# A hybrid encoder layer: two blocks at a time through the MLP, or one block with the next block's mixers between its steps

## The chip, the cores and the metric

The kernel runs on one core of a Trainium2 chip. The metric is the device time of one execution in microseconds (us). The engines are TensorE (PE, matmuls; PEld is its weight load), VectorE (DVE), ScalarE (ACT), GpSimd (POOL) and SyncE (SP), whose queue issues nearly all DMAs. SBUF is the memory on chip, PSUM the eight banks that matmuls write to.

## What is computed

One layer over 2,176 tokens of width 1024: a prompt of 2,048 and 8 running streams of 16 new frames. All data are fp32. The reference, cut down:

```python
h = rmsnorm(x, ln_mix)
q, k, v, u = split(h @ w_in)                  # 512, 128, 128, 512 columns
a = attention(q, k, v)                        # 8 heads, 2 kv heads; own 64-frame chunk + 128 frames before, sinks
b = multiscale_pool(u) * pool_scale           # trailing means over 2/4/8/16 frames minus u, 4 linear maps
x = x + concat(rmsnorm(a), rmsnorm(b)) @ w_out
x = x + square(relu(rmsnorm(x) @ w_up)) @ w_down          # 4096 hidden columns
x = x + sigmoid(rmsnorm(x) @ w_gate) * (p @ w_ple)
y = rmsnorm(x)                                # also returned: K, V and pooling rows
```

## The kernel before

Activations lie transposed, features on the 128 partitions and tokens along the row. The tokens are cut into six blocks (`BLOCKS`): block 0 has 256 (128 of the prompt and the 128 sample frames), the others 384. Blocks depend on each other only through the last 128 keys and values and the last 15 pooling rows of the block before.

Precision is kept by splitting each operand into a rounded part and the rest, hi and lo; each product is three matmuls (`mm3`, L113: hi x hi, lo x hi, hi x lo). `load_w` (L101) brings a 128 x 1024 weight tile of 512 KB by DMA into one of two raw buffers (`wraw`), ACT casts it to `whi` (L107), and DVE and POOL in turn subtract to give `wlo` (L110); there are three pairs of hi and lo. A tile feeds 24 matmuls for each block that uses it.

Phase A works off `SEQ_A`, an order written out by hand: for each block the norm and split of x (`P`), the input projection in 10 tiles (`I`), the attention in tiles of 128 queries (`A`; `S` for the sample streams of block 0), pooling (`K`), and the output projection (`O`), whose result x1 is written to HBM (`x1d`, L239). Blocks overlap in it. K and q have two buffers, the pooling input `ext` one.

Phase B takes the blocks in pairs, `SUPER = [(1, 2), (3, 4), (5, 0)]`. `mlp_start` reads x1 back, norms and splits it; `acc_load` reads it once more as the accumulator. `mlp` (L649) runs 16 chunks of two up-tiles and two down-tiles. Each weight tile is loaded and split once and used for both blocks. An up-tile ends in r = relu(ps) * rstd on DVE (L662), hi = square(r) on ACT (L666), r*r on DVE (L667) and lo = r*r - hi on DVE (L668). A down-tile's eight outputs are added to the accumulator in SBUF by DVE (L682), 128 adds a block. PSUM tiles of the MLP rotate through seven banks. Then come `gate` (L692) for each of the two, with the sigmoid and its multiplication, and `finish`, with the last norm and the output. All gate weights are split by POOL.

Instructions go out in an order that a planner in the compiler draws up from simulated times: an instruction later in the program can come ahead of one that is not ready. On the chip each engine then keeps its order.

Of the kernel before, what the change touches and what calls it, by code (L numbers as in the profile page):

```python
# [43 lines left out]
FCH = 2  # L44
# [8 lines left out]
C_W = 53  # L53


@with_exitstack
def hymba_step(ctx: ExitStack, tc: tile.TileContext, ins, outs):
# [34 lines left out]
    RING = ("mm", "sc", "tr", "mm", "sc", "tr", "pv")  # L92
    ring = [0]

    def ps_ring(nm):
        ring[0] += 1
        return ps_tile(RING[ring[0] % len(RING)], nm)

    cnt = [0]

    def load_w(src, ktiles, width=P, raw_bufs=2, hl_bufs=3, tag="w", pool=None, eng=None):  # L101
        pool = pool or wp
        raw = pool.tile([P, ktiles, width], F32, tag=tag + "r", name="wraw", bufs=raw_bufs)
        nc.sync.dma_start(out=raw, in_=src)
        hi = pool.tile([P, ktiles, width], F32R, tag=tag + "h", name="whi", bufs=hl_bufs)
        lo = pool.tile([P, ktiles, width], F32R, tag=tag + "l", name="wlo", bufs=hl_bufs)
        nc.scalar.copy(out=hi, in_=raw)  # L107
        cnt[0] += 1
        eng = eng or (nc.vector if cnt[0] % 2 else nc.gpsimd)
        eng.tensor_tensor(out=lo, in0=raw, in1=hi.bitcast(F32), op=ALU.subtract)  # L110
        return hi, lo

    def mm3(ps, whl, xs, first=True, last=True):  # L113
        n = len(xs)
        hi, lo = whl
        for i, (wsel, (xh, xl)) in enumerate(xs):
            nc.tensor.matmul(ps, lhsT=wsel(hi), rhs=xh, start=first and i == 0, stop=False)  # L117
            nc.tensor.matmul(ps, lhsT=wsel(lo), rhs=xh, start=False, stop=False)  # L118
            nc.tensor.matmul(ps, lhsT=wsel(hi), rhs=xl, start=False, stop=last and i == n - 1)  # L119

    def ks(xt, N, kk):
        return [((lambda t, k=k: t[:, k, :]), (xt[0][:, k, :N], xt[1][:, k, :N])) for k in kk]
# [5 lines left out]
    class SumSq:  # L128
        def __init__(self, n, acc=None):
            self.n = n  # L130
            self.acc = acc if acc is not None else tmp.tile([P, NMAX], F32, tag="sqa", name="sqa", bufs=5)
            self.first = True
            self.last_sig = None
# [31 lines left out]
        def rstd_load(self, dim, pstile):  # L165
# [27 lines left out]
    def row_tile(nm):  # L193
        return tmp.tile([P, NMAX], F32, tag="xr", name=nm, bufs=NXR)

    def load_norm(b, src, g, hl, rstd):
        N = BLOCKS[b]
        sq = SumSq(N)
        for k in range(KT):
            x = row_tile("x")[:, :N]  # L200
            nc.sync.dma_start(out=x, in_=src[:, k, :])
            gain_split(x, g + k, hl[0][:, k, :N], hl[1][:, k, :N], LOENG[k % len(LOENG)](nc))
            sq.add(x, eng=ADENG[k % len(ADENG)](nc))
        return rstd(sq)

    def hl_tile(nm, pool=xhl):
        h = pool.tile([P, KT, NMAX], F32R, tag="xh", name=nm + "h")
        l = pool.tile([P, KT, NMAX], F32R, tag="xl", name=nm + "l")
        return h, l
# [674 lines left out]
```

## Time and profile before

| | |
|---|---|
| median of 3 runs | 2560.95 us (2559.33 to 2562.33) |
| span of the profiled execution | 2563.4 us |
| busy: PE, DVE, ACT, POOL | 2438.7, 1814.0, 874.2, 827.8 us |
| DMA traffic | 249.17 MB, 97 GB/s on average |
| granted PE clock, mean | 0.977 |

A busy time is the union of an engine's instructions. Matmuls overlap in the record, so a busy PE is not yet a PE at its peak pace; the pace is seen by counting matmuls in a stretch. The idle time of an engine that is not the bound costs nothing.

### The profile page before, as it was taken

The page shows a single profiled execution, that of the slowest core. Times are in us where ns is not written, and L with a number is a line of the kernel's source. Part 1 is how long each engine was busy: PE and PEld are TensorE (multiplying, and loading weights), DVE is VectorE, ACT ScalarE, POOL GpSimd, SP SyncE. Part 2 cuts the span into 40 slices and gives each one's busy share as a digit, 9 for nine tenths or more (in the row PEclk, how much of TensorE's full clock was granted, in tenths as well). Part 3 has the DMA queues.
Part 4 walks back from the last instruction along what each step waited for, and adds up shares of the span by engine and source line. Part 5 has one row for each costly group of instructions (what it writes and reads, how often), then busy time and mean ns, then how long its engine had stood idle before and what let it go on. Part 6 is the DMA issues. An engine that isn't in the chain of part 4 may idle for free.

```text
span 2563.4 us, 36604 instructions
## 1 busy us (share of the span) xinstructions
PE 2438.7 (95%) x14324; PEld 2361.4 (92%) x14324; DVE 1814.0 (71%) x3113; ACT 874.2 (34%) x1601; POOL 827.8 (32%) x548
## 2 busy tenths in 40 slices
PE   7889998999899999999998999999999899999986
PEld 7888888998799999999888999999988899999986
DVE  6769888888765555555889555555587966666687
ACT  5446655445421111111652111111165212221254
POOL 4634557454631111111381111111138211111134
PEclk8989999999999999999999999999999999999998
DMA  5424335433732222222244222221234422222223
GB/s 157 129 87 137 95 120 165 138 106 97 249 102 65 59 66 66 63 62 66 91 151 158 66 66 59 66 63 59 61 102 135 136 75 75 83 74 67 83 76 113
DMA packets 104892, 249.17 MB, mean 97 GB/s; under 512 B 19600, under 2 KB 55440, under 8 KB 104720
## 3 DMA queue, kind: packets, MB, share of 16 engines
q1 hardware_dynamic: 104176, 246.32, 31.4%
q8 instruction: 112, 1.84, 0.3%
q10 hardware_dynamic: 544, 0.52, 0.1%
q14 instruction: 60, 0.49, 0.1%
HBM read 228.44 MB, written 18.36 MB: 96 GB/s over the span
## 4 chain that ended last, share of the span: by engine, by line
PE 59%; DVE 10%; ACT 2%; DMA 2%; issue 1%; POOL 0%; SPq 0%; DVEq 0%; ACTq 0%; POOLq 0%
PE ps_dn L117 10%; PE ps_dn L118 10%; PE ps_dn L119 10%; PE ps_up L119 9%; PE ps_up L118 9%; PE ps_up L117 9%; DVE sqa L144 2%; DVE acc L714 1%; DVE x1l L191 1%; DVE x2l L191 1%; DMA x<-x1d 1%; DVE rs_t L159 1%; DMA xr<-in_xT 1%; ACT whi L107 1%; DVE acc L737 1%
## 5 line engine op out<-in xcount | busy, mean ns | idle before, releaser
L110 POOL TENSOR_TENSOR wlo<-wraw,whi 128x1024 fp32r<-128x1024 f32 (+1 forms) x245 | 533.0, 2182 | 1466.9 <-ACT whi L107 1452.1
L107 ACT CAST whi<-wraw 128x1024 fp32r<-128x1024 f32 (+1 forms) x395 | 377.1, 968 | 999.8 <-issue 578.5
L682 DVE TENSOR_TENSOR acc<-ps_dn,acc 128x384 f32<-128x384 f32 (+1 forms) x768 | 389.6, 530 | 167.9 <-PE ps_dn L119 166.9
L117 PE MATMUL ps_dn<-hh,whi 128*128 128x384 f32 (+1 forms) x1536 | 500.0, 327 | 4.5 <-DVE r L662 4.5
L119 PE MATMUL ps_up<-x1l,whi 128*128 128x384 f32 (+1 forms) x1536 | 501.0, 326 | 1.2 <-DVE x1l L191 1.2
L117 PE MATMUL ps_up<-x1h,whi 128*128 128x384 f32 (+1 forms) x1536 | 501.4, 327 | 0.7 <-ACT x1h L190 0.7
L118 PE MATMUL ps_up<-x1h,wlo 128*128 128x384 f32 (+1 forms) x1536 | 501.9, 327 | 0.0
L118 PE MATMUL ps_dn<-hh,wlo 128*128 128x384 f32 (+1 forms) x1536 | 499.4, 327 | 0.0
L119 PE MATMUL ps_dn<-hl,whi 128*128 128x384 f32 (+1 forms) x1536 | 488.0, 326 | 0.0
L117 PEld LDWEIGHTS ps_dn<-hh,whi 128*128 128x128 f32 x1536 | 290.8, 189 | 5.1 <-DVE r L662 5.1
L119 PEld LDWEIGHTS ps_up<-x1l,whi 128*128 128x128 f32 x1536 | 290.2, 189 | 2.0 <-DVE x1l L191 1.5
L117 PEld LDWEIGHTS ps_up<-x1h,whi 128*128 128x128 f32 x1536 | 290.1, 189 | 1.3 <-ACT x1h L190 1.0
L118 PEld LDWEIGHTS ps_up<-x1h,wlo 128*128 128x128 f32 x1536 | 290.3, 189 | 0.7 <-issue 0.6
L118 PEld LDWEIGHTS ps_dn<-hh,wlo 128*128 128x128 f32 x1536 | 290.8, 189 | 0.0
L119 PEld LDWEIGHTS ps_dn<-hl,whi 128*128 128x128 f32 x1536 | 289.0, 189 | 0.2 <-DVE hl L668 0.2
L662 DVE SCALAR_TENSOR_TENSOR r<-ps_up,sqa 128x384 f32<-128x384 f32 x192 | 102.1, 535 | 254.2 <-PE ps_up L119 254.0
L667 DVE TENSOR_TENSOR r<-r 128x384 f32<-128x384 f32 x192 | 191.2, 998 | 97.4 <-ACT hh L666 97.4
L110 DVE TENSOR_TENSOR wlo<-wraw,whi 128x1024 fp32r<-128x1024 f32 x150 | 191.0, 1273 | 56.4 <-ACT whi L107 54.1
L666 ACT ACTIVATE hh<-r 128x384 fp32r<-128x384 f32 x192 | 96.3, 504 | 300.2 <-DVE r L662 300.0
L117 PE MATMUL ps_in<-xnh,whi 128*128 128x384 f32 (+1 forms) x472 | 162.9, 345 | 12.9 <-DVE z L561 5.5
L118 PE MATMUL ps_in<-xnh,wlo 128*128 128x384 f32 (+1 forms) x472 | 161.2, 342 | 2.7 <-POOL wlo L110 2.0
L119 PE MATMUL ps_in<-xnl,whi 128*128 128x384 f32 (+1 forms) x472 | 159.6, 339 | 0.0
(208 smaller groups left out, 3992.4 us busy)
## 6 DMA issues: line engine op xcount, KB each, us to landing
wraw<-in_w_up SPq DMA_DIRECT2D x96, 512.0 KB, 3.7
wraw<-in_w_down SPq DMA_DIRECT2D x96, 512.0 KB, 3.6
wraw<-in_w_in SPq DMA_DIRECT2D x59, 512.0 KB, 3.7
wraw<-in_w_out SPq DMA_DIRECT2D x48, 512.0 KB, 3.7
wraw<-in_w_gate SPq DMA_DIRECT2D x48, 512.0 KB, 3.6
x<-in_xT SPq DMA_DIRECT2D x40, 192.0 KB, 2.6
xr<-in_xT SPq DMA_DIRECT2D x40, 192.0 KB, 3.2
x1d<-xr SPq DMA_DIRECT2D x40, 192.0 KB, 2.1
```

The costliest lines, as they stand in the source:

```text
L107: nc.scalar.copy(out=hi, in_=raw)
L110: eng.tensor_tensor(out=lo, in0=raw, in1=hi.bitcast(F32), op=ALU.subtract)
L117: nc.tensor.matmul(ps, lhsT=wsel(hi), rhs=xh, start=first and i == 0, stop=False)
L118: nc.tensor.matmul(ps, lhsT=wsel(lo), rhs=xh, start=False, stop=False)
L119: nc.tensor.matmul(ps, lhsT=wsel(hi), rhs=xl, start=False, stop=last and i == n - 1)
L144: eng.tensor_tensor(out=o, in0=o, in1=t, op=ALU.add)
L159: V.tensor_tensor(out=u, in0=u, in1=y, op=ALU.mult)
L191: eng.scalar_tensor_tensor(out=lo, in0=src, scalar=c, in1=hi.bitcast(F32), op0=ALU.mult, op1=ALU.subtract)
L662: nc.vector.scalar_tensor_tensor(out=r, in0=ps, scalar=0.0, in1=rs1[b], op0=ALU.max, op1=ALU.mult)
L666: nc.scalar.activation(out=hh, in_=r, func=AF.Square)
L667: nc.vector.tensor_tensor(out=r, in0=r, in1=r, op=ALU.mult)
L682: nc.vector.tensor_tensor(out=acc[b][:, d, :N], in0=ps, in1=acc[b][:, d, :N], op=ALU.add)
```

## The change

Blocks now go through the MLP one at a time, 0 to 5. Block 0 first passes all its mixers and its output projection alone. Then, between the 64 steps (32 up-tiles, 32 pairs of down outputs) of block b's MLP, `run` places the steps of block b+1: reading and splitting x, 10 projection tiles, pooling groups, attention tiles in four steps each. In `gate` of block b the eight output tiles of block b+1 are placed; they start two tiles ahead of it. `out_proj` writes x1 into the accumulator and its split form on chip, so `x1d` and its transfers are gone.

The MLP has 8 chunks of four up-tiles; `w_down` is packed anew on the host so that a 512 KB tile holds two outputs for four hidden tiles. A block has 64 adds into the accumulator. r*r is on POOL.

Up and down weights are loaded and split for every block. The weights of input, output, gate and embedding projections are split at their first use, stored to HBM as hi and lo, and loaded as these from then on, two DMAs of 512 KB.

Large tiles of a block come from one pool of 16 buffers of 4 x 384 columns (`quad`). K and `ext` have one buffer. Of the PSUM banks four are for projections, MLP and gate, and one each for scores, transposes, values and sums. The adds of squares and the gate's add to the accumulator are on POOL; before, those of phase B were on DVE. The diff, cut to its core:

```diff
-SUPER = [(1, 2), (3, 4), (5, 0)]
-FCH = 2
+FCH = 4
+NCH = FT // FCH
+NQUAD = 16
+PS_BUFS = {"mm": 4, "sc": 1, "tr": 1, "pv": 1, "ms": 1}
...
-    def load_w(src, ktiles, width=P, raw_bufs=2, hl_bufs=3, tag="w", pool=None, eng=None):
+    def load_w(src, ktiles, key=None, raw_bufs=2, hl_bufs=3, tag="w", pool=None, eng=None):
...
+        if key in saved:
+            dh, dl = saved[key]
+            nc.sync.dma_start(out=hi.bitcast(F32), in_=dh)
+            nc.sync.dma_start(out=lo.bitcast(F32), in_=dl)
+            return hi, lo
...
+        if key is not None:
+            dh, dl = (dram.tile([P, ktiles, P], F32, name=f"ws{key}{c}") for c in "hl")
+            nc.sync.dma_start(out=dh, in_=hi.bitcast(F32))
+            nc.sync.dma_start(out=dl, in_=lo.bitcast(F32))
+            saved[key] = dh, dl
...
+    def out_proj(b, d):
...
+        a = acc_at(b, d)
+        nc.sync.dma_start(out=a, in_=xblk(xT, KT, b)[:, d, :])
+        whl = load_w(w_out[d], KT, f"out{d}")
...
+        gain_split(a, C_GFFN + d, at8(x1[b][0], d)[:, :N], at8(x1[b][1], d)[:, :N], nc.vector)
+        st_b["sq1"].add(a)
+        if d == KT - 1:
+            rs1[b] = st_b["sq1"].rstd_dve(D)
...
+        def up(c, j):
+            if j == 0:
+                hs[c] = quad("hh", F32R), quad("hl", F32R)
+            whl = load_w(w_up[c * FCH + j], KT)
+            ps = ps_tile("mm", "ps_up")[:, :N]
+            mm3(ps, whl, ks(x1[b], N, range(KT)))
+            r = row_tile("r")[:, :N]
+            nc.vector.scalar_tensor_tensor(out=r, in0=ps, scalar=0.0, in1=rs1[b], op0=ALU.max, op1=ALU.mult)
+            hh, hl = hs[c][0][:, j, :N], hs[c][1][:, j, :N]
+            nc.scalar.activation(out=hh, in_=r, func=AF.Square)
+            nc.gpsimd.tensor_tensor(out=r, in0=r, in1=r, op=ALU.mult)
+            nc.vector.tensor_tensor(out=hl, in0=r, in1=hh.bitcast(F32), op=ALU.subtract)
...
+            for i in range(2):
...
+                d = 2 * dp + i
+                ps = ps_tile("mm", "ps_dn")[:, :N]
+                mm3(ps, whl, [(i * FCH + j, (hh[:, j, :N], hl[:, j, :N])) for j in range(FCH)])
+                a = acc_at(b, d)
+                nc.vector.tensor_tensor(out=a, in0=ps, in1=a, op=ALU.add)
...
+    for b in range(nb):
+        nx = b + 1
+        side = []
+        if nx < nb:
+            side = prologue_steps(nx) + in_proj_steps(nx)
+            mix = [s for i in range(NPR[nx] // P) for s in attn_steps(nx, i)]
+            for i, s in enumerate(pool_steps(nx)):
+                mix.insert(3 * i, s)
+            side += [lambda: mixers(nx)] + mix + [lambda: out_rstd(nx)]
+        run(mlp_steps(b), side, 1, 62)
+        gate_rs(b)
+        G = [lambda d=d: gate(b, d) for d in range(KT)]
+        if nx < nb:
+            out_proj(nx, 0)
+            out_proj(nx, 1)
+            run(G, [lambda d=d: out_proj(nx, d) for d in range(2, KT)])
+        else:
+            run(G)
+        finish(b)
```

## Rows read from the trace of the kernel before

**Rows 1.** Busy time by stretch: us; busy us (count) per engine; clock, DMA share, GB/s.

```profile
0.00:200.00 200.00, 170.00 (x932) 156.74 (x933) 143.38 (x287) 94.24 (x203) 100.89 (x96) 0.89 0.45 125
200.00:640.00 440.00, 425.84 (x2427) 382.87 (x2427) 386.00 (x836) 242.59 (x561) 230.77 (x189) 0.99 0.40 123
640.00:724.00 84.00, 70.30 (x364) 64.98 (x362) 62.98 (x79) 37.16 (x63) 55.21 (x41) 0.94 0.67 231
724.00:1243.00 519.00, 519.00 (x2994) 518.70 (x2993) 310.32 (x489) 105.44 (x150) 77.75 (x32) 1.00 0.22 66
1243.00:1344.00 101.00, 89.26 (x493) 84.71 (x492) 87.48 (x104) 63.34 (x110) 73.99 (x46) 1.00 0.43 129
1344.00:1390.00 46.00, 37.05 (x191) 35.80 (x190) 44.82 (x84) 9.81 (x17) 8.29 (x3) 0.89 0.34 120
...
2025.00:2455.00 430.00, 430.00 (x2942) 430.00 (x2941) 281.22 (x484) 95.45 (x138) 74.71 (x31) 1.00 0.26 78
2455.00:2518.00 63.00, 54.81 (x312) 52.95 (x312) 49.39 (x67) 36.48 (x64) 35.49 (x21) 0.92 0.35 103
2518.00:2563.40 45.40, 25.50 (x178) 23.48 (x176) 33.55 (x56) 16.75 (x34) 16.55 (x11) 0.80 0.30 102
```

**Rows 2.** Score matmuls by tile, one of three such lines: ns, first and last.

```profile
L391 PE MATMUL ps_sc<-kh,qh x128: 271/280/579, 29.3 to 626.6; 64*128 64x256 f32 x120, 64*128 64x128 f32 x8
```

**Rows 3.** Weight splitting, groups by shape: count, busy us, mean ns, idle before.

```profile
L110 POOL TENSOR_TENSOR wlo<-wraw,whi 128x1024 fp32r<-128x1024 f32 x197 | 483.6, 2456 | 1440.6 <-ACT whi L107 1425.7 <-DVE sbuf L479 8.3 <-DMA wraw<-in_w_out 3.8
...
L107 ACT CAST whi<-wraw 128x1024 fp32r<-128x1024 f32 x347 | 359.1, 1048 | 999.8 <-issue 578.5 <-PE ps_up L119 245.8 <-PE ps_dn L119 55.1
...
L110 DVE TENSOR_TENSOR wlo<-wraw,whi 128x1024 fp32r<-128x1024 f32 x150 | 191.0, 1273 | 56.4 <-ACT whi L107 54.1 <-issue 0.6
```

**Rows 4.** Loads of up weights, from the page's DMA issues: KB, us to landing.

```profile
wraw<-in_w_up SPq DMA_DIRECT2D x96, 512.0 KB, 3.7
```

**Rows 5.** ACT in order of time, 20 to 46 us: first and last of six casts.

```profile
22.38 1.04 ACT L107 CAST whi<-wraw 128x1024 fp32r<-128x1024 f32 x1
...
43.41 1.04 ACT L107 CAST whi<-wraw 128x1024 fp32r<-128x1024 f32 x1 [1.10 <-DMA wraw<-in_w_in]
```

**Rows 6.** Busy time by stretch: the stretch with the densest DMA traffic.

```profile
684.00:688.00 4.00, 4.00 (x24) 3.84 (x23) 1.69 (x2) 1.33 (x2) 4.00 (x4) 1.00 1.02 421
```

**Rows 7.** Page's groups of the MLP steps, then two groups by shape.

```profile
L682 DVE TENSOR_TENSOR acc<-ps_dn,acc 128x384 f32<-128x384 f32 (+1 forms) x768 | 389.6, 530 | 167.9 <-PE ps_dn L119 166.9
...
L662 DVE SCALAR_TENSOR_TENSOR r<-ps_up,sqa 128x384 f32<-128x384 f32 x192 | 102.1, 535 | 254.2 <-PE ps_up L119 254.0
L667 DVE TENSOR_TENSOR r<-r 128x384 f32<-128x384 f32 x192 | 191.2, 998 | 97.4 <-ACT hh L666 97.4
...
L666 ACT ACTIVATE hh<-r 128x384 fp32r<-128x384 f32 x192 | 96.3, 504 | 300.2 <-DVE r L662 300.0
...
L668 DVE TENSOR_TENSOR hl<-r,hh 128x384 fp32r<-128x384 f32 x160 | 92.3, 578 | 4.1
...
L235 POOL TENSOR_TENSOR xr<-xr,ot 128x384 f32<-128x384 f32 x40 | 45.4, 1135 | 98.7 <-DVE ot L234 75.9 <-DMA xr<-in_xT 6.7 <-DVE st L415 6.3
```

**Rows 8.** In order of time around 729 us; then L667's min, median, max.

```profile
728.90 2.43 DVE L667 TENSOR_TENSOR r<-r 128x384 f32<-128x384 f32 x2
...
728.03 2.40 POOL L110 TENSOR_TENSOR wlo<-wraw,whi 128x1024 fp32r<-128x1024 f32 x1 [5.67 <-ACT whi L107]
...
L667 DVE TENSOR_TENSOR r<-r x192: 416/559/2440, 719.1 to 2442.4; 128x384 f32<-128x384 f32 x160, 128x256 f32<-128x256 f32 x32
```

**Rows 9.** Block 0's pooling and sample streams: count, ns, first and last start us.

```profile
L323 POOL TENSOR_TENSOR pw<-ext x2: 1177/2107/3037, 63.2 to 81.3; 128x960 f32<-128x960 f32 x1, 128x568 f32<-128x568 f32 x1
...
L468 PE MATMUL ps_ssc<-sbuf x16: 283/284/580, 115.3 to 170.1; 128*128 128x144 f32 x16
...
L491 ACT COPY asm<-ps_str x16: 201/207/209, 128.9 to 185.5; 64x64 f32<-64x64 f32 x16
```

**Rows 10.** PE in order of time near the end: the last gate matmul.

```profile
2549.37 0.28 PE L119 MATMUL ps_gt<-x2l,whi 128*128 128x256 f32 x1
```

More of the change, by code (lines that the diff above doesn't have):

```diff
@@ L115, in mm3, with ks @@
         hi, lo = whl
[L116 to L122, printed above, removed]
+        for i, (wi, (xh, xl)) in enumerate(xs):
+            nc.tensor.matmul(ps, lhsT=hi[:, wi, :], rhs=xh, start=first and i == 0, stop=False)
+            nc.tensor.matmul(ps, lhsT=lo[:, wi, :], rhs=xh, start=False, stop=False)
+            nc.tensor.matmul(ps, lhsT=hi[:, wi, :], rhs=xl, start=False, stop=last and i == n - 1)
+    def ks(xt, N, kk, w0=0):
+        return [(w0 + i, (at8(xt[0], k)[:, :N], at8(xt[1], k)[:, :N])) for i, k in enumerate(kk)]
     def split(src, hi, lo, lo_eng):
@@ L163, in rstd_dve, with rstd_load @@
             return v
[L165 removed]
+        def rstd_load(self, dim):
             last = self.last_sig if self.last_sig is not None else self.last
@@ L193, in row_tile @@
     def row_tile(nm):
[L194 to L209, printed above, removed]
+        return tmp.tile([P, NMAX], F32, tag="xr", name=nm, bufs=4)
@@ new lines, in prologue_steps, with part, rs @@
+    def prologue_steps(b):
+        N = BLOCKS[b]
+        st_b = state[b] = {}
+        src = xblk(xT, KT, b)
+        def part(k0):
+            if k0 == 0:
+                st_b["xn"], st_b["sq"] = hl_pair("xn"), SumSq(N)
+            xn = st_b["xn"]
+            for k in range(k0, k0 + 2):
+                x = row_tile("x")[:, :N]
+                nc.sync.dma_start(out=x, in_=src[:, k, :])
+                gain_split(x, C_GMIX + k, at8(xn[0], k)[:, :N], at8(xn[1], k)[:, :N], nc.vector)
+                st_b["sq"].add(x)
+        def rs():
+            st_b["rs"] = st_b["sq"].rstd(D)
+        return [lambda k0=k0: part(k0) for k0 in range(0, KT, 2)] + [rs]
@@ new lines, in one, with mixers @@
+                        out=exs[:, g, :, HIST : HIST + TDEC],
+                        in0=ps[:, NP:N].rearrange("p (s q) -> p s q", s=NSTREAM),
+                        in1=rs[:, NP:N].rearrange("p (s q) -> p s q", s=NSTREAM),
+                        op=ALU.mult,
+                    )
+        return [lambda e=e: one(e) for e in range(10)]
+    def mixers(b):
+        st_b = state[b]
+        st_b["mx"] = hl_pair("mx")
+        st_b["sqb"] = SumSq(BLOCKS[b])
+        st_b["sqa"] = SumSq(BLOCKS[b])
@@ new lines, in finish, with run @@
+    def finish(b):
+        N = BLOCKS[b]
+        rs = sqs[b].rstd_load(D)
+        for k in range(KT):
+            a = acc_at(b, k)
+            nc.vector.scalar_tensor_tensor(
+                out=a, in0=a, scalar=cv_sb[:, C_GFIN + k : C_GFIN + k + 1], in1=rs, op0=ALU.mult, op1=ALU.mult,
+            )
+            (nc.scalar if b == nb - 1 and k % 2 else nc.sync).dma_start(out=xblk(yT, KT, b)[:, k, :], in_=a)
+    def run(main, side=(), lo=0, hi=None):
+        hi = len(main) if hi is None else hi
+        n = len(side)
+        at = [lo + (i * (hi - lo)) // n for i in range(n)]
+        j = 0
+        for i, step in enumerate(main):
+            step()
+            while j < n and at[j] <= i:
+                side[j]()
+                j += 1
+        while j < n:
+            side[j]()
+            j += 1
@@ new lines, in hymba_step @@
+    prologue0()
+    consts()
+    for step in in_proj_steps(0):
+        step()
+    mixers(0)
+    for step in attn_steps(0, 0):
+        step()
+    pool0()
+    attn_sample(0, NPR[0])
+    out_rstd(0)
+    for d in range(KT):
+        out_proj(0, d)
+    for b in range(nb):
[14 more added lines that the diff above has]
+            run(G, [lambda d=d: out_proj(nx, d) for d in range(2, KT)])
+        else:
+            run(G)
+        finish(b)
```

975 lines of the change are left out of this document (434 added, 541 removed).

## The prediction

> **What bounds the kernel now.** I read the busy time by stretch first, with the stretches cut where TensorE (PE) changes stage [rows 1]. In the two-block MLP, PE is busy 100% at granted clock 1.00: 2994 matmuls in 519 us, 173 ns each for 384 columns. The last pair mixes 384 and 256 columns: 2942 in 430 us, 146 ns on average, so 119 ns for 256 columns (2 x 146 - 173). Nothing but PE bounds those stretches; VectorE (DVE) is at 60%, GpSimd (POOL) at 15%.
>
> These two paces price all of PE's work. A block has 2,208 matmuls of its own width by the code (240 in, 192 out, 1536 MLP, 240 gate), and 12 of pooling. Five blocks: 5 x 2220 x 0.1733 = 1,924 us; block 0: 2208 x 0.119 = 263 us. Scores are 3 x 128 x 0.119 = 46 [rows 2]; the values are 186 by the code, of 512 columns, 0.231 us by proportion, 43; transposes, sums, the sample streams and block 0's pooling add about 70 by their columns (estimate). Sum 2,346 us. The span is 2563.4, so **217 us are lost**, and they are all outside the MLP. From counts against length of each stretch in [rows 1]: start to 200 us 59; 200 to 640, where projections and attention alternate, 44 of 440 (DVE 88% busy); 640 to 724, the switch to the MLP, 20; each change of pair 27 (twice; 101 + 46 us for 493 + 191 matmuls); the end 37. The clock row says the same: 0.89 at the start, 0.80 at the end, 1.00 in the MLP.
>
> **The change, part by part.** PE's matmuls are the same ones, so the new time is 2,346 plus new losses. The terms:
>
> 1. *Start.* Block 0 now goes alone through projection, attention, pooling, samples and output projection before any MLP step; what filled PE before (blocks 1 and 2) is placed later, and block 1's projection cannot come forward, because K and the pooling input have one buffer each. Chain: weights arrive every 4.2 us at the start (casts 22.38 to 43.41 in five intervals [rows 5]: 3.7 us to land [rows 4], 1.05 cast, 1.27 on DVE or 2.46 on POOL to subtract [rows 3], two raw buffers). Now each of them is also stored as two 512 KB halves behind it in SP's queue; 1.57 MB per weight at the 421 GB/s of the busiest stretch [rows 6] is 3.7 us, so the stores fit, but the next load is queued behind them: I take 4.8 us, projection done at 63 us. Pooling of block 0 ran from 63 us to where the first sample's scores begin, 115, amid block 1's work, and the samples from there to 185.5 [rows 9]. Alone I take 32 and 40 us (bounds: the 52 and 70 measured, or half of them), hence 135 us. Output projection: 23 us of PE, eight weights, most of them at 4.5 us; overlapped with the samples' end, the MLP begins at **155** (135 to 190). Useful PE work in it is 68 us, so the loss is 87.
>    PE idles here, and in [rows 1] its clock falls where it idles (0.89 over the first 200 us). The Trainium skill ("TensorE: Matmul & The Clock Gate", Part 1: The HAM clock gate) says that an idle PE drops to half its clock until it has been busy again; the trace agrees. By that rule the 23 us of output projection would be 46, which is more than the 36 of its weights, and the start 10 us longer; that is inside the bounds above.
> 2. *Side work in the MLP.* 15 attention tiles, 5 projections and the poolings are spread over 5 MLPs. In 200 to 640 some 12 tiles lost 44 us, 3.7 each, with DVE nearly full. Now DVE has less: 32 splits of 1.27, 32 x (0.54 + 0.58) and 64 x 0.53 for the MLP [rows 3, 7], and for three tiles with all that goes with them at most 3 x 386/12 = 97 [rows 1], together 208 us of a stretch of 345. So I take 1.1 us a tile, **16** (bounds 5 and 55). One score bank and one transpose bank instead of two stand behind that upper bound.
> 3. *Chunks of four.* Half of the accumulating adds go (768 to 384 x 0.53 = 204 us of DVE) and the 192 squares r*r leave DVE (191 us) for POOL, at 1.1 us by POOL's add of the same shape [rows 7]. DVE is not the bound, so this saves nothing directly. It costs where the fourth up-tile feeds the first down: 0.54 + 0.50 + 1.1 + 0.58, some 3 us with hops [rows 7]. Before, the other block's 4.1 us of matmuls lay there; now PE has only the first three tiles' share of the next outputs, 9 matmuls or 1.6 us each, in four banks: up to 6 us if they are ordered so. 48 chunks at 0.4 us: **20** (0 to 90; the upper end is rival 2).
> 4. *Weights for one block.* Up and down are loaded and split six times, not three: 384 raw loads, not 192. All other weights are split once and then come back as halves without ACT, DVE or POOL. Per pair of raw weights the POOL buffer takes 3.7 + 1.05 + 2.46 + hops = 7.5 us, some 8.1 with queueing: 4.05 a weight. A 384-block consumes one in 24 x 0.173 = 4.16. Blocks 1 to 4 have side work of 10 projections (42 us of PE), three tiles of about 8 (24 score, 12 value matmuls and transposes) and sums, near 75 us, so 5.3 a weight: nothing. In block 5 without side work: **4** (0 to 30). Block 0 consumes one in 2.86, with block 1's side work 253/64 = 3.95; 64 x 4.05 = 259 plus some waits of SP's queue, where a returning half must wait for its slot and the next raw load behind it: **18** (6 to 55).
> 5. *Gate with output projection.* No splitting there any more, and outputs of the next block fill PE while the gate's norm is made. Sixteen weights of 1.05 MB and 5 MB of embeddings, x and y in 75 us are 300 GB/s, under the 421 seen [rows 6]. A change of pair lost 27; without its reloads and its POOL load (74 of 101 us busy) I take 5.5 at each of four, **22** (8 to 40), and **10** at the first (4 to 25), whose gate weights are still split, and stored.
> 6. *x1 on chip.* 108 transfers through HBM go, and with them the 20 us at 640 to 724. Nothing more: in the MLP the DMA share is 0.22.
> 7. *End.* One gate of 384 columns. From the last gate matmul (2549.4 [rows 10]) to the end were 14 us at 256 columns; wider, and with two of its adds on POOL: 18, plus 6 for the norm ahead of the gate: **24** (18 to 35).
>
> Sum: 2346 + 87 + 16 + 20 + 4 + 18 + 22 + 10 + 24 = **2547 us** of span. The profiled span is 2.4 us above the median of the three runs, so I say 2545, 0.6% below. Its own range is 2515 to 2578.
>
> **Rivals.**
> - *A: the fill is nearly perfect* (2465 to 2515). The ordered stretch from 300 us on already lost little, with twice the attention per us. Start at 145 (77), tiles 8, chunks 8, supply 5, gates 13, end 20: 2,477. Against: chains across four engines, and a POOL three times as busy. Chance 0.20.
> - *B: the weights become the bound* (slower). Place: the raw buffer's cycle in single-block MLPs. For: 4.2 us at the start with little queued [rows 5], against 4.16 needed; POOL has squares and sums in front of its subtractions now. At 4.6 us a weight, block 0 takes 64 x 4.6 = 294 (41 lost, not 18) and block 5 294 (28, not 4): 2547 + 47 = 2,594. It decides from 4.35 us a weight on, where the two lose 15 us more. Chance 0.17.
> - *C: the POOL square holds the chunk* (slower). In [rows 8] two DVE squares that began inside a POOL subtraction (728.03 to 730.43) took 2.43 us and ended after it, and the longest single square took 2.44 against a median of 0.56. If each chunk's last hl waits out such a subtraction, 48 x 1.88 = 90 us instead of 20: 2,617; at half of them 2,575. It decides from 0.75 us a chunk. The Trainium skill ("SBUF — State Buffer", "Who interferes with whom") says that a DVE instruction with two SBUF inputs and a POOL instruction that reads SBUF exclude each other for their whole length; by that rule the move to POOL puts one more holder into this chain, and the row agrees. Against C: DVE does not wait so every time, only when POOL's subtraction lies there (4 in 33 us). Chance 0.15.
> - *D: the start is long*, MLP at 190: 2,582. Chance 0.10.
> - The forecast: 0.38.
>
> That the steps are not placed as written is possible, since a planner orders the instructions, but it would change where a loss sits, not the list.
>
> **How the numbers follow.** About 0.2% (5 us) is what a measurement can tell. The forecast's range splits 0.24 faster, 0.07 the same, 0.07 slower; A is faster; B gives 0.02, 0.01, 0.14; C 0.03, 0.02, 0.10; D 0.01, 0.01, 0.08. Faster 0.50, same 0.11, slower 0.39. The range takes A's middle and C's full price: 2475 to 2622.
>
> **What would show it.** Step 1: first up-matmul near 155 us. Steps 2 and 3: granted clock 1.00 and PE busy above 97% in the MLPs; waits of down matmuls on hl under 20 us in all. Step 4: casts no further apart than 4.2 us in block 5. Step 5: no gap above 6 us where blocks change. The prediction is wrong if weights or hl head the list of what PE waits for, or if PE's busy share in the MLPs falls under 95%.

## The result, and the profile after

The changed kernel takes a median of 2593.78 us (2592.89 to 2600.62, four runs) against 2560.94 of the kernel before in the same session: ratio 1.013, 95% interval 1.0114 to 1.0146. It is **1.3% slower**; 0.6% faster was predicted. The profiled span is 2591.2 us. Medians here are of fast executions; of the four of the run spread below, one of 7471.64 us is left out.

The busy time by stretch, cut at the first up matmul and the first gate matmul of each block, with the first 40 us of the MLPs of blocks 1 and 2 cut off (columns as in [rows 1]):

```profile
0.00:177.00 177.00, 107.71 (x587) 89.77 (x587) 85.54 (x228) 57.05 (x138) 56.69 (x66) 0.74 0.64 187
177.00:474.60 297.60, 281.18 (x2003) 267.78 (x2004) 179.70 (x345) 129.27 (x235) 151.33 (x112) 0.97 0.55 175
474.60:536.30 61.70, 57.00 (x388) 55.61 (x387) 30.63 (x44) 24.33 (x44) 46.31 (x40) 0.97 0.90 335
536.30:576.30 40.00, 33.00 (x160) 30.71 (x159) 33.31 (x48) 19.56 (x34) 22.95 (x17) 0.83 0.49 154
576.30:900.10 323.80, 323.80 (x1852) 314.34 (x1850) 173.86 (x308) 115.82 (x204) 132.49 (x92) 1.00 0.45 144
900.10:966.80 66.70, 66.70 (x386) 66.70 (x386) 27.64 (x47) 19.32 (x35) 29.22 (x28) 1.00 0.70 240
966.80:1006.80 40.00, 32.53 (x170) 31.25 (x169) 32.98 (x45) 19.49 (x31) 20.67 (x15) 0.91 0.46 147
1006.80:1329.90 323.10, 322.08 (x1840) 312.31 (x1839) 173.90 (x308) 114.77 (x202) 134.33 (x94) 1.00 0.45 144
...
2255.70:2532.20 276.50, 272.05 (x1542) 267.82 (x1542) 126.57 (x187) 88.22 (x113) 124.93 (x72) 0.99 0.43 130
2532.20:2591.20 59.00, 44.20 (x245) 42.46 (x244) 19.33 (x35) 16.42 (x27) 18.36 (x18) 0.90 0.47 161
```

Of the whole, the page's busy times and its traffic, for the table that stands ahead of [rows 1]:

```profile
PE 2449.6 (95%) x14324; PEld 2366.3 (91%) x14324; DVE 1377.9 (53%) x2434; ACT 930.7 (36%) x1627; POOL 1133.1 (44%) x843
...
DMA packets 154177, 425.93 MB, mean 164 GB/s; under 512 B 25232, under 2 KB 61328, under 8 KB 154000
```

DVE has 436 us less to do than before, POOL 305 more, and the traffic is up by 177 MB. No engine but PE is near its limit, so the averages don't tell where the time went.

Read the stretches as [rows 1]: length against the matmuls in it at 173 or 119 ns. The gates of blocks 1 to 4 are full (386 x 0.173 = 66.8 of 66.7 us, clock 1.00), and nearly so is the MLP from 40 us behind a change of block on (1852 x 0.173 = 320 of 323.8 us). What is not full: the start, the first MLP (183 us for its 1536 up and down matmuls, 42 for 240 projections and about 36 for the rest, of 297.6), and **the first 40 us behind each change**: 160 and 170 matmuls there are 27.7 and 29.5 us, at clock 0.83 and 0.91. With 2,346 us of work the 2591.2 hold 245 us of loss:

| place | predicted loss | measured |
|---|---|---|
| start (first up matmul at 155; came at 177.0) | 87 | 105.1 |
| MLP of block 0 (weights 18, side work 3, chunks 3) | 24 | 36.7 |
| gates of block 0 | 10 | 7.8 |
| the four changes: gates of blocks 1 to 4 | 22 | 0.4 |
| the four changes: first 40 us of the MLPs 1 to 4 | none of its own | 43.4 |
| rest of the MLPs 1 to 4 (side work, chunks) | 26 | 26.1 |
| MLP of block 5 (weights 4, chunks 3) | 7 | 9.0 |
| last gate and end | 24 | 16.1 |

What PE waited for, over the whole run (us in total, times, longest):

```profile
PE ps_dn L126 <- DVE hl L664: 38.8, 13, 7.3
PE ps_b L124 <- ACT mxh L132: 26.2, 2, 19.7
PE ps_in L124 <- ACT whi L109: 6.5, 2, 6.3
```

Most of the first line is the block change (31.7 of its 38.8 us; the other 7.1 fall in block 0's MLP): hl heads the list, which the prediction named as a sign of its being wrong. DVE in order of time behind the last gate matmul of block 1:

```profile
968.46 0.56 DVE L710 TENSOR_TENSOR sg<-ps_ple,sg 128x384 f32<-128x384 f32 x1 [0.95 <-ACT sg L709]
971.07 0.56 DVE L160 TENSOR_SCALAR sqa<-ps_ms 128x384 f32<-128x384 f32 x1 [2.05 <-PE ps_ms L156]
...
977.32 2.64 DVE L165 SCALAR_TENSOR_TENSOR rs_t<-sqa,rs_t 128x384 f32<-128x384 f32 x1
979.99 0.56 DVE L166 TENSOR_TENSOR rs_t<-rs_t 128x384 f32<-128x384 f32 x1
980.58 0.56 DVE L167 SCALAR_TENSOR_TENSOR sqa<-rs_t 128x384 f32<-128x384 f32 x1
981.25 1.02 DVE L660 SCALAR_TENSOR_TENSOR r<-ps_up,sqa 128x384 f32<-128x384 f32 x2
...
986.31 7.13 DVE L720 SCALAR_TENSOR_TENSOR acc<-acc,cv_sb,sqa 128x384 f32<-128x384 f32 x8
993.37 0.54 DVE L664 TENSOR_TENSOR hl<-r,hh 128x384 fp32r<-128x384 f32 x1
```

The eleven operations of rs1, the norm factor that each up-tile's r needs, run from 971.07 to 981.14; PE had its first up matmul at 966.8 and had more than three up-tiles done when the first r came, at 981.25. Then the final scaling of the block before (L720, eight in one go) takes 7.13 us ahead of the hl of 993.37, for which PE waits 7.3 us. What this hl reads of POOL was done by 984.4, so the place in VectorE's queue kept it, not POOL:

```profile
982.44 1.93 POOL L663 TENSOR_TENSOR r<-r 128x384 f32<-128x384 f32 x2 [2.90 <-ACT hh L662]
```

Of the 10.5 us lost in these first 40 us of block 2, the wait is 7.3. The rest is mostly pace: after the wait, in which PE did nothing, its granted clock was 0.50 (the lower level, 1.2 GHz) and then 0.67, and 23 matmuls kept it busy for 6.0 us instead of 4.0:

```profile
992.00:996.00 4.00, 2.03 (x6) 2.00 (x7) 3.86 (x8) 0.52 (x1) 0.92 (x1) 0.50 0.96 307
996.00:1000.00 4.00, 4.00 (x17) 4.00 (x17) 2.88 (x5) 2.44 (x5) 1.95 (x3) 0.67 0.80 281
```

In the start the queues show the same pattern with DMA ahead of it. ACT in order of time, and the loads from issue to landing in 0 to 177 us:

```profile
59.44 0.59 ACT L132 CAST ph<-ps_tr 128x512 fp32r<-128x512 f32 x1
68.30 1.04 ACT L109 CAST whi<-wraw 128x1024 fp32r<-128x1024 f32 x1 [8.28 <-DMA wraw<-in_w_out]
69.25 0.59 ACT L455 ACTIVATE at<-ps_pv 128x512 f32<-128x512 f32 x1
```

```profile
wraw<-in_w_in SPq DMA_DIRECT2D x9, 512.0 KB, 5.4
wraw<-in_w_out SPq DMA_DIRECT2D x8, 512.0 KB, 6.7
```

The cast stood waiting for a weight until 68.30, and the attention's result, which PE had finished by 64.5, was read behind it (L455, 69.25). These loads take 5.4 and 6.7 us to land; those of w_up took 3.7 before [rows 4].

### The profile page after: what moved, and what is told of

Same layout as the page of the kernel before. It is cut to its first block, busy times and chain, and to the rows that moved or that the text cites. A ratio compares the mean times of both kernels' runs of the same rounds, so it can differ in the third digit from the quotient of the medians.

```text
span 2591.2 us, 37319 instructions
## 1 busy us (share of the span) xinstructions
PE 2449.6 (95%) x14324; PEld 2366.3 (91%) x14324; DVE 1377.9 (53%) x2434; ACT 930.7 (36%) x1627; POOL 1133.1 (44%) x843
## 4 chain that ended last, share of the span: by engine, by line
PE 80%; DVE 6%; DMA 4%; POOL 3%; issue 2%; ACT 1%; SPq 0%; POOLq 0%; DVEq 0%; ACTq 0%
PE ps_dn L124 9%; PE ps_dn L125 9%; PE ps_dn L126 9%; PE ps_up L124 8%; PE ps_up L125 8%; PE ps_up L126 8%; PE ps_in L124 3%; PE ps_in L125 3%; PE ps_in L126 3%; PE ps_gt L124 2%; PE ps_gt L125 2%; PE ps_gt L126 2%; POOL wlo L112 2%; PE ps_pv L536 1%; DVE acc L720 1%
## 5 line engine op out<-in xcount | busy, mean ns | idle before, releaser
L112 POOL TENSOR_TENSOR wlo<-wraw,whi 128x1024 fp32r<-128x1024 f32 (+1 forms) x216 | 519.0, 2404 | 805.3 <-ACT whi L109 769.0
L109 ACT CAST whi<-wraw 128x1024 fp32r<-128x1024 f32 (+1 forms) x417 | 429.7, 1036 | 900.3 <-PE ps_up L126 287.0
L126 PE MATMUL ps_dn<-hl,whi 128*128 128x384 f32 (+1 forms) x1536 | 490.9, 334 | 38.9 <-DVE hl L664 38.8
L124 PE MATMUL ps_dn<-hh,whi 128*128 128x384 f32 (+1 forms) x1536 | 506.3, 335 | 5.8 <-DVE acc L678 1.8
L125 PE MATMUL ps_dn<-hh,wlo 128*128 128x384 f32 (+1 forms) x1536 | 506.6, 332 | 2.6 <-DVE wlo L112 2.6
L112 DVE TENSOR_TENSOR wlo<-wraw,whi 128x1024 fp32r<-128x1024 f32 x201 | 277.6, 1381 | 107.3 <-ACT whi L109 105.4
L124 PEld LDWEIGHTS ps_dn<-hh,whi 128*128 128x128 f32 x1536 | 294.6, 193 | 16.2 <-DVE acc L678 7.6
L678 DVE TENSOR_TENSOR acc<-ps_dn,acc 128x384 f32<-128x384 f32 (+1 forms) x384 | 192.3, 528 | 182.5 <-PE ps_dn L126 182.2
L663 POOL TENSOR_TENSOR r<-r 128x384 f32<-128x384 f32 (+1 forms) x192 | 198.6, 1038 | 199.7 <-ACT hh L662 199.7
L660 DVE SCALAR_TENSOR_TENSOR r<-ps_up,sqa 128x384 f32<-128x384 f32 (+1 forms) x192 | 101.6, 532 | 238.9 <-PE ps_up L126 237.2
L151 POOL TENSOR_TENSOR sqa<-sqa,sqt 128x384 f32<-128x384 f32 (+1 forms) x161 | 178.6, 1110 | 113.1 <-ACT sqt L150 110.2
L664 DVE TENSOR_TENSOR hl<-r,hh 128x384 fp32r<-128x384 f32 (+1 forms) x192 | 135.3, 707 | 124.0 <-POOL r L663 122.7
```

What stands on the lines that cost most here:

```text
L124: nc.tensor.matmul(ps, lhsT=hi[:, wi, :], rhs=xh, start=first and i == 0, stop=False)
L125: nc.tensor.matmul(ps, lhsT=lo[:, wi, :], rhs=xh, start=False, stop=False)
L126: nc.tensor.matmul(ps, lhsT=hi[:, wi, :], rhs=xl, start=False, stop=last and i == n - 1)
L151: eng.tensor_tensor(out=o, in0=o, in1=t, op=ALU.add)
L660: nc.vector.scalar_tensor_tensor(out=r, in0=ps, scalar=0.0, in1=rs1[b], op0=ALU.max, op1=ALU.mult)
L663: nc.gpsimd.tensor_tensor(out=r, in0=r, in1=r, op=ALU.mult)
```

## The experiments

The losses by place, worked out as above for every run (blocks 2 to 4 together; "first 40" is the mean over blocks 1 to 5 and is contained in the MLP columns; not listed: the end, 16 us in each, and the gates of blocks 1 to 4, 0.1 us each, but 4.0 for block 1 in store_third and 6.0 in best_store). They are those of the one profiled execution, which in no_first_store, best_store and best_sq0 is some 4 us faster than the median:

| kernel | start | MLP and gates 0 | MLP 1 | MLPs 2 to 4 | MLP 5 | first 40 | median us | ratio to before (95%) |
|---|---|---|---|---|---|---|---|---|
| changed kernel | 105.1 | 44.5 | 18.1 | 51.4 | 9.0 | 9.9 | 2593.78 | 1.0130 (1.0114 to 1.0146) |
| no_first_store | 84.9 | 68.5 | 15.0 | 52.1 | 9.0 | | 2598.04 | 1.0157 (1.0138 to 1.0177) |
| early_out | 103.2 | 43.6 | 18.5 | 52.0 | 5.4 | 9.7 | 2585.60 | 1.0098 (1.0083 to 1.0113) |
| square_dve | 102.2 | 40.1 | 18.0 | 61.5 | 5.4 | | 2592.65 | 1.0127 (1.0112 to 1.0142) |
| samples4 | 88.4 | 45.6 | 17.8 | 51.4 | 9.0 | | 2578.33 | 1.0068 (1.0052 to 1.0084) |
| late_finish | 103.1 | 43.0 | 18.5 | 52.5 | 10.6 | 9.5 | 2592.67 | 1.0118 (1.0101 to 1.0135) |
| early_late | 103.1 | 41.9 | 16.0 | 51.0 | 5.4 | 9.1 | 2587.13 | 1.0094 (1.0077 to 1.0110) |
| store_third | 86.1 | 50.3 | 23.7 | 56.7 | 10.5 | | 2596.40 | 1.0134 (1.0118 to 1.0149) |
| start4 | 84.2 | 46.1 | 17.0 | 49.7 | 10.6 | | 2572.97 | 1.0045 (1.0030 to 1.0061) |
| spread | 101.7 | 46.0 | 18.5 | 48.1 | 5.0 | 2.3 | 2581.42 | 1.0072 (1.0055 to 1.0089) |
| spread_early | 102.4 | 44.9 | 13.0 | 41.5 | 3.3 | 0.4 | 2570.97 | 1.0035 (1.0025 to 1.0046) |
| best | 81.9 | 46.7 | 15.1 | 42.8 | 3.4 | 0.4 | 2552.46 | 0.9959 (0.9945 to 0.9974) |
| best_store | 65.3 | 63.5 | 11.1 | 41.2 | 3.3 | 0.4 | 2559.32 | 0.9985 (0.9975 to 0.9994) |
| half_w0 | 101.6 | 27.6 | 18.2 | 53.7 | 10.3 | | 2575.40 | 1.0054 (1.0039 to 1.0069) |
| best_sq0 | 84.4 | 47.3 | 14.0 | 42.1 | 3.3 | | 2559.28 | 0.9987 (0.9978 to 0.9997) |

**The write-backs.** The weights of the input and output projections are stored one block later, and so split once more, in the second block:

```diff
-        if key is not None:
+        if key is not None and not in_start[0]:
...
     for d in range(KT):
         out_proj(0, d)
+    in_start[0] = False
```

> Weights of the input and output projections are split in the first block without being written back; the write-back moves to the second block's use of them. Theory (the write-backs stand ahead of the raw loads in SP's queue and lengthen the start): the first up matmul comes at 160 to 168 us instead of 177.0, the raw loads of w_in and w_out land in about 4 us instead of 5.4 and 6.7, and the time falls from 2594 to 2578 to 2587, with 2 to 3 us given back in the first block's MLP, where the splitting now lies. Rival (the start is a chain of small dependent steps, and the loads only wait beside it): first up matmul at 174 or later, time 2591 to 2598.

The first up matmul came at 156.8, earlier than the theory's 160, and the loads landed in 4.0 and 5.1 us: the write-backs do lengthen the start, by 20 us (13.5 of them in the projection, done at 50.3 us instead of 63.8). But the time didn't fall; the next stretches of this run, in the second and third row, show why:

```profile
0.00:156.80 156.80, 106.18 (x588) 89.47 (x588) 87.05 (x223) 55.60 (x137) 55.30 (x64) 0.74 0.36 96
156.80:464.50 307.70, 286.95 (x2006) 269.33 (x2006) 195.93 (x355) 143.93 (x251) 163.91 (x120) 0.97 0.57 183
464.50:540.20 75.70, 62.48 (x387) 58.71 (x386) 38.65 (x51) 29.86 (x50) 49.68 (x40) 0.93 0.93 330
```

The gates of block 0, which already write back the gate weights, took 75.7 us instead of 61.7, at a DMA share of 0.93, and the MLP 10 more. So I moved the writes to the third block (`save=b == 2` in `load_w`, both calls):

> The split weights of the input and output projections are written back when the third block splits them instead of the first; the first two blocks split them raw. Theory (the write-backs cost some 20 us wherever SP's queue and the DMA engines have no room, in the start as in the first gates): the first up matmul at 157 to 160 us, as with the write-back one block later, but the gates of block 0 lose 8 to 14 us instead of 22 and the first MLP 36 to 42 instead of 46, since nothing is written there; the third block's use lies in a 384-column MLP and its gates and costs under 4 us; time 2572 to 2584. Rival (it is the splitting on ACT, VectorE and POOL that costs, not the writes): the first MLP and its gates lose as much as with the write-back one block later, 2588 to 2598.

The start again gained 19, and block 0 gave back 6 only, but MLP 1 5.6, its gates 3.9, MLPs 2 to 4 5.3 and MLP 5 1.5: 22 in all. The theory's time was wrong, and the rival's number right for another reason: the weights are now also split twice more, and this work, with the writes, found no free place in any of the blocks where it fell. Which of the two costs more there these runs don't tell.

**The samples.** The eight streams' stages are issued for four streams at a time, in eight banks; each `yield` ends a stage:

```diff
-        for s in range(NSTREAM):
-            ps = ps_tile("sc", "ps_ssc")
+        def stream(s):
+            o = ps_tile("mm", "ps_ssc")[:, :NKEY]
...
+            tp = ps_tile(("sc", "tr", "ms", "pv")[s % 4], "ps_str").rearrange("p (t q) -> p t q", t=NQT)
...
+        for s0 in range(0, NSTREAM, 4):
+            for _ in zip(*(stream(s) for s in range(s0, s0 + 4))):
+                pass
```

> The eight sample streams run in two groups of four, stage by stage, in eight PSUM banks instead of one after the other in two banks. Theory (the start is a chain of small dependent steps): the stretch from the first to the last sample matmul falls from 42.5 us to 24 to 30, the first up matmul from 177.0 to 159 to 167, the time to 2574 to 2585. Rival (their work on TensorE at half clock and on VectorE fills the stretch already): 38 us or more, time within 4 us of 2594.

As the theory had it. The copy of each stream's result on ACT, by tile (ns min, median, max; first and last start), in the changed kernel and then here:

```profile
L592 ACT COPY asm<-ps_str x16: 194/206/208, 109.8 to 143.6; 64x64 f32<-64x64 f32 x16
```

```profile
L595 ACT COPY asm<-ps_str x16: 206/208/209, 106.4 to 125.3; 64x64 f32<-64x64 f32 x16
```

From the first score (102.5 and 99.1) to the last copy 41 us became 26, the first up matmul came at 160.3, and the time fell by 15 us.

Then pooling's sums and splits ahead of the samples, its matmuls and scaling behind them (the `yield`s in `pool_mix4` part the two):

```diff
-    pool0()
+    p0 = pool0()
+    next(p0)
     attn_sample(0, NPR[0])
+    next(p0)
```

> The four-at-a-time samples, and besides the pooling's sums and splits ahead of the samples with its matmuls and scaling behind them. Theory (in the start TensorE waits for one chain after the other): the 28 us of idle time ahead of the pooling's matmuls go to the sample matmuls, first up matmul at 145 to 152 instead of 160.3 with the samples alone, time 2562 to 2570. Rival (the pooling's sums on POOL hold VectorE's queue, and with it the samples): 157 or later, 2574 to 2582.

156.1 and 2573: between the two. The first sample matmul now starts at 86.2, but PE idles 21.2 us ahead of it. DVE in order of time:

```profile
76.35 1.22 DVE L112 TENSOR_TENSOR wlo<-wraw,whi 128x1024 fp32r<-128x1024 f32 x1 [7.14 <-ACT whi L109]
77.49 0.69 DVE L429 SCALAR_TENSOR_TENSOR dt<-pw,ext 128x128 f32<-128x128 f32 x3
...
85.54 0.60 DVE L562 TENSOR_TENSOR sbuf<-qh,ql 64x64 f32<-64x64 f32 x2
```

A weight's subtraction waited 7.14 us for its cast, and the cast for a DMA in SP's queue; pooling and the samples stood behind it. The profile names the store of the pooling rows there, not the weight's load:

```profile
75.27 1.04 ACT L109 CAST whi<-wraw 128x1024 fp32r<-128x1024 f32 x1 [7.01 <-DMA out_pool_s_out<-ext]
```

**The square on POOL (rival C).** `nc.vector` for `nc.gpsimd` in L663.

> r*r of the up step goes back to VectorE. Theory (POOL's square is late only where POOL is behind, at block changes): waits of the down matmuls on hl (38.8 us in 13 waits) fall by a third, time 2578 to 2592. Rival (the square on POOL holds the last hl of every chunk): the waits on hl vanish and the time falls below 2570. Other rival (VectorE is the scarcer engine in the side work): 2597 or more.

No change in time. The waits on hl fell from 38.8 to 14.6 us, by more than the theory's third, and a wait on r took their place:

```profile
PE ps_dn L124 <- DVE r L660: 27.4, 5, 8.0
...
PE ps_dn L126 <- DVE hl L664: 14.6, 13, 2.4
```

So the square isn't what holds the chunk, and rival C's price of 1.88 us at each of 48 chunks isn't there. MLPs 2 to 4 lose 10 us more with it on DVE.

**The block change.** First the output projections of the next block earlier, so that rs1 is:

```diff
-            run(G, [lambda d=d: out_proj(nx, d) for d in range(2, KT)])
+            run(G, [lambda d=d: out_proj(nx, d) for d in range(2, KT)], 0, 4)
```

> The eight output projections of the next block are placed ahead of gate 4 instead of ahead of gate 7. Theory (the first chunk after a block change loses some 10 us since rs1, a chain of POOL additions, a matmul and eleven VectorE operations, begins too late): rs1 is ready before the last gate matmul, the losses in the first 40 us of each of the blocks 1 to 5 fall from about 10 to 3 to 5 us, and the time to 2562 to 2578. Rival (VectorE's finishing multiplications and POOL's queue hold the first chunk whatever rs1 does): 2586 to 2596.

The theory fell: rs1 was in time and the 40 us lost as much as before, but for the change into block 5, whose MLP has no next block's work: it loses 3.6 us less. The profiled spans differ by 5.5 us in all, the medians by 8. DVE at a change, where the first up matmul was at 1394.6:

```profile
1390.82 0.56 DVE L167 SCALAR_TENSOR_TENSOR sqa<-rs_t 128x384 f32<-128x384 f32 x1
...
1398.99 0.56 DVE L660 SCALAR_TENSOR_TENSOR r<-ps_up,sqa 128x384 f32<-128x384 f32 x1 [1.56 <-PE ps_up L126]
...
1415.18 2.72 DVE L191 SCALAR_TENSOR_TENSOR sqa<-sqa,rs_t 128x384 f32<-128x384 f32 x1
...
1418.83 7.12 DVE L720 SCALAR_TENSOR_TENSOR acc<-acc,cv_sb,sqa 128x384 f32<-128x384 f32 x8
1425.87 1.66 DVE L197 SCALAR_TENSOR_TENSOR xnl<-x,cv_sb,xnh 128x384 fp32r<-128x384 f32 x3
1427.45 0.55 DVE L664 TENSOR_TENSOR hl<-r,hh 128x384 fp32r<-128x384 f32 x1
```

r now waits for PE, as it should, but the chunk's last hl comes no earlier: the final norm (L191), its eight multiplications and the splits of the next block's input (L197) stand ahead of it, probably since they are ready earlier. So I issued the multiplications later, between steps 8 and 22 of the next MLP, alone and with the early output projections:

> The eight finishing multiplications of a block (L720) and its output's stores are issued between up and down steps 8 to 22 of the next block's MLP instead of ahead of it. Theory, as it stands after the runs so far (two things hold the first chunk after a block change, each enough by itself: rs1's chain, and VectorE's backlog of the final scaling's multiplications ahead of the last hl): alone it gains little, the first 40 us of the blocks 1 to 5 still lose 8 to 11 us each, time 2583 to 2593. Rival (VectorE's finishing work alone holds it): 3 to 5 us each, time 2560 to 2575.

> Both edits: output projections of the next block ahead of gate 4, and the final scaling between the steps 8 to 22 of the next MLP. Theory (two causes, each enough by itself): the first 40 us of the blocks 1 to 5 lose 3 to 6 us instead of 10 to 12, time 2552 to 2572. Rival (a third cause: the first side steps, the next block's input splits on VectorE and ACT and their additions on POOL, and the final rstd): they lose 8 or more, time 2578 to 2586.

Neither changed the 40 us, but the edit didn't take effect. In the second of the two the multiplications (L724 here) still lie ahead of the last hl:

```profile
1413.95 7.13 DVE L724 SCALAR_TENSOR_TENSOR acc<-acc,cv_sb,sqa 128x384 f32<-128x384 f32 x8
1421.01 1.66 DVE L197 SCALAR_TENSOR_TENSOR xnl<-x,cv_sb,xnh 128x384 fp32r<-128x384 f32 x3
1422.59 0.55 DVE L664 TENSOR_TENSOR hl<-r,hh 128x384 fp32r<-128x384 f32 x1
```

The planner had pulled them forward; these two runs say nothing on the cause. With ordering edges it holds (the multiplications one by one behind the hl of the next two chunks, the side work from step 8 on):

```diff
+        def behind(f, t=FCH - 1):
+            def g():
+                with tc.issue_after(anchor[b, t]):
+                    f()
+            return g
...
+            fin = [behind(lambda: finish_rs(b - 1))]
+            fin += [behind(lambda k=k: finish(b - 1, k), FCH + k) for k in range(KT)]
...
+        side = [behind(f) for f in side[:4]] + side[4:]
+        run(M, side, 8, 62)
```

> In the two kernels with the late final scaling the trace still has the eight multiplications ahead of the first chunk's last hl (1413.95 to 1420.5 against 1422.6): the planner pulled them forward. Here ordering edges put them, the final rstd and the next block's input splits behind the first chunk's last hl on VectorE, the multiplications one by one behind the hl of the second and third chunk. Output projections stay where the changed kernel has them (ahead of gate 7). Theory (rs1's chain and VectorE's backlog each hold the first chunk): rs1 still does, the first 40 us of the blocks 1 to 5 lose 7 to 10 us, time 2575 to 2590. Rival (VectorE's backlog alone): 3 to 6 us, 2562 to 2574.

> The same edges, and the output projections ahead of gate 4. Theory (both causes gone): the first 40 us of the blocks 1 to 5 lose 3 to 6 us instead of 10 to 12, no wait of the first down matmuls on hl above 2 us, time 2552 to 2570. Rival (POOL's weight subtractions of 2.4 us between its squares hold the last hl): still 8 or more, time 2576 to 2588.

With the edges alone the 40 us lose 2.3 instead of 9.9: in this the rival was nearer, VectorE's backlog was the larger cause, and rs1's lateness costs 2 us. The edges also hold back what ACT and POOL do for the same steps; that it was VectorE's part is shown by the row of 982.44, not by these runs. And the time fell only to 2581: of the 7.6 us saved at a change some 6.5 came back later in the same MLP (MLPs 2 to 4 lose 48.1 against 51.4). With both edits 0.4 is left of the 40 us, and the time falls by 23 us to 2571, 1 us above the theory's range; of 47 us taken out at the five changes 21 stay saved (MLPs 1 to 5 lose 57.8 instead of 78.5). The second of these kernels, first 40 us of block 2 and the rest:

```profile
959.90:999.90 40.00, 39.88 (x229) 39.29 (x228) 17.48 (x27) 15.69 (x21) 19.67 (x13) 1.00 0.39 121
999.90:1318.70 318.80, 314.21 (x1781) 303.64 (x1780) 184.62 (x316) 118.42 (x214) 135.99 (x97) 0.99 0.47 149
```

229 matmuls in 40 us is the full pace; the 4.6 idle us behind them are where the postponed work now lies.

**Both together**, the early output projections and edges with the start of start4, and the same with the write-backs at the third block:

> The edges and the early output projections together with the start of the run before (samples four at a time, pooling around them). Theory (the losses of the start and of the block changes are separate and add up): start 156, first 40 us of the blocks 3 to 6 us, time 2530 to 2550, under the kernel before. Rival (what is saved in one place comes back as backlog in the next, as the deferred write-backs did): 2555 or more.

> The kernel of the run before this one, with the input and output projections' weights written back at the third block's use instead of the first. Theory (in that start the write-backs hold the raw loads, these ACT's casts, and these VectorE's queue, 7.1 us at once): first up matmul at 130 to 140 instead of 156, of which 15 to 22 us come back at the second and third block's MLP and gates, so the time stays within 8 us of the run before. Rival (with the block changes eased, the later stages have room for the writes): 10 to 20 us faster.

The first is 0.4% faster than the kernel before and 41 us under the changed kernel, 2.5 us above the theory's range: the gains add up (21 from the start, 23 from the changes). In the second the first up matmul comes at 137.2, and block 0's MLP and gates lose 63.5 instead of 46.7: 16.6 us gained, 16.8 given back there. Here too the write-backs only change place: the profiled spans are 0.6 us apart, and the median is 7 us above the first's.

**Block 0's MLP.** Every second weight left out:

```diff
-            whl = load_w(w_up[c * FCH + j], KT)
+            if b or j % 2 == 0:
+                hs["w"] = load_w(w_up[c * FCH + j], KT)
+            whl = hs["w"]
```

(and so in `down`).

> The changed kernel, but in the first block's MLP every second weight tile is not loaded: two up steps, and two down steps, use the same one (a part of that block's weights is left out, so its numbers are other ones). Theory (the first block's MLP lost 36.7 us, twice the forecast, since its 256-column matmuls use up a weight every 2.9 us of their own work, and loads, casts and subtractions for it share the engines with the side work): the loss in that stage falls to 15 to 22, time 2572 to 2582. Rival (chains of the side work and of rs1 hold it): it stays at 30 or more, time 2585 to 2594.

> The fastest version so far (early output projections, edges, samples four at a time), with r*r on VectorE in the first block alone. Theory (POOL, which squares, subtracts and adds, is behind in that block): its MLP loses 30 to 34 us instead of 38.4, time 2545 to 2551. Rival (VectorE becomes as late as POOL was): 37 or more, 2551 to 2557.

With half the weights the MLP of block 0 loses 23.1 instead of 36.7 (1 us more than the theory's range), its gates 4.5 instead of 7.8, and the time falls by 18 us: the supply is most of what was over the forecast. Which link of it (load, cast, subtraction) was not tried. Moving the square of this block to VectorE made the MLP 7 us shorter (31.1 against 38.4) and the gates behind it 8 longer (16.2 against 8.3): nothing gained, and the median is 7 us above that of best.

## Why the prediction was wrong, step by step

- **Step 5, the change of block, is the step that failed**: "I take 5.5 at each of four". Its two parts were right, the gates are full and lose 0.1 each. What it didn't ask was what the next MLP needs first: rs1, and a VectorE free of the block before. Each change cost 11 us (43.4 over four), in the first 40 us of the next MLP. What the runs show in place of the 5.5 is, at three of the four, a wait of 7.3 us on an hl that VectorE came to late, and a slower PE behind it. spread_early takes the loss out of that place, and about 4 us of each stay saved; that the rest comes back through the postponed work is read from where that work lies, and was not tested.
- **Step 1, the start**, was mis-sized: 105 us, not 87. The projection was done when forecast (63 us; 63.8 measured). Pooling and the attention tile then took 38.7 us instead of 32, the samples 40.9 instead of 40, and the output projection, which overlapped with nothing, 33.6 instead of 20, which is most of what was missed. The stores cost 20 us. Of these 13.5 lie in the projection, whose end the forecast still hit: it had put 0.6 us a weight on them, 6 in all, so this hit is partly luck. Without them (no_first_store) pooling and the attention tile take as long, 38.5, the samples 38.8 and the output projection 29.2, so the stores, of which the step says "so the stores fit", explain some 6 of the 22 us by which the first up matmul was late. The samples were a chain by their issue order, 15 us of which went with four at a time; the forecast had that chain in its 40 us.
- **Step 4, the weights**: right for block 5 (9.0 us, 6.0 of it in the first 40), so rival B didn't happen at its price; for block 0 18 became about 30. With half its weights left out, that MLP and its gates lose 17 us less (half_w0), so most of the excess is supply. PE's busy share in that MLP was 94.5% (281.18 of 297.60 us), under the 95% that the prediction named as a sign of being wrong.
- **Steps 2 and 3** hold in size: the MLPs 1 to 4 behind their first 40 us lose 26.1, as the 26 summed. This agreement is partly luck: with the changes eased, the same stretches lose more (52.9 over the four in spread_early), probably since the work that stood in the first chunk then falls there. And the waits on hl are 38.8, not under 20; 31.7 of them sit at block changes, none recurs at each chunk, and square_dve shows that POOL's square is no cause of time (rival C, whose price at half the chunks adds up to 2572, not 2575). The lock that stood behind C is there: L165 at 977.32 took 2.64 us instead of 0.56 beside a POOL subtraction (977.06 for 2.49). The Trainium skill ("SBUF — State Buffer", "Who interferes with whom") has it so, and this trace agrees; it lengthens rs1's chain by 2 us. More hangs on it in the burst for which hl waits: one of the eight multiplications took 2.69 us beside a weight subtraction on POOL, against a median of 0.605, and the eight 7.13, where eight at 0.605 are at most 4.84. So some 2 us of the 7.3 us wait (an estimate from these figures) come from it, most of them beside POOL's subtraction, and none beside its square.

```profile
987.58 2.69 DVE L720 SCALAR_TENSOR_TENSOR acc<-acc,cv_sb,sqa 128x384 f32<-128x384 f32 x1
987.21 2.65 POOL L112 TENSOR_TENSOR wlo<-wraw,whi 128x1024 fp32r<-128x1024 f32 x1
L720 DVE SCALAR_TENSOR_TENSOR acc<-acc,cv_sb,sqa x48: 473/605/2689, 561.5 to 2587.7; 128x384 f32<-128x384 f32 x40, 128x256 f32<-128x256 f32 x8
```

- **Step 7**, the end, was better than forecast (16.1, not 24), block 0's gates too (7.8, not 10). Step 6 has no loss of its own.

Start +18, block 0 +12, the changes +22, the end and the first gates -10, small ones +2: 44 us, which is what lies between 2547 and the span of 2591.

## What to carry to other kernels

When one block's work is to fill another's gaps, price the first chunk behind each change by what its operands need on every engine's queue, and not only by whether PE has work; work that is ready early and needed late must be held behind urgent work by an ordering edge, as a new place in the program didn't move it here. Traffic that is moved out of a crowded stretch saves time only if the place it goes to has room on the queue, the DMA engines and the splitting engines; measure the whole, since the 17 to 20 us saved at the start came back in full, three times.

## What the runs showed of the hardware

- Through the samples PE's granted clock was 0.50 of full speed, the lower level (1.2 GHz), in the changed kernel, with PE busy in 27.84 of 42.50 us. In start4 it was still 0.50 with PE busy in 23.80 of 29.20, and in samples4 0.56 with 23.02 of 26.40, where it rose only at the end (0.50 up to 119 us). Closer packing made the chain shorter, and hardly the clock faster. The rows are of the changed kernel, start4 and samples4:

```profile
102.50:145.00 42.50, 27.84 (x84) 17.44 (x84) 19.82 (x89) 11.54 (x52) 1.43 (x3) 0.50 0.08 22
```

```profile
86.20:115.40 29.20, 23.80 (x84) 17.46 (x84) 17.30 (x92) 10.08 (x49) 0.00 (x0) 0.50 0.24 75
```

```profile
99.10:125.50 26.40, 23.02 (x86) 17.22 (x86) 14.37 (x76) 9.82 (x48) 0.29 (x1) 0.56 0.09 26
```

- A 512 KB load lands in 3.6 us (median) in the MLPs, in 5.4 and 6.7 us where 512 KB stores are issued on the same queue, and in 4.0 and 5.1 in the same stretch without these stores.
